# A 90-degree rotation: loads split over two queues, and one transpose per slab in place of two

## The chip, the cores and the metric

The kernel runs on one core of one Trainium2 chip (trn2). The metric is the device time of one execution in microseconds (us), lower is better. The profiled executions had a granted clock of 1.00. "The same" means a difference under 2%.

Names: SyncE and ScalarE issue transfers here and do nothing else. VectorE ("DVE" in the profile) does the transposes. "DMA" is the core's 16 DMA engines, which move the bytes of every transfer, whoever issued it. HBM is the chip's main memory and SBUF the core's own, where the tiles lie. The span is the profiled stretch, from the first to the last instruction.

## The reference

```python
def setup_inputs():
    batch, c, h, w = 32, 3, 256, 256
    return {"x": np.random.randn(batch, c, h, w).astype(np.float32)}

def reference(x):
    return np.rot90(x, k=-1, axes=(-2, -1)).astype(np.float32)
```

There are 96 planes of 256 x 256 float32, each rotated clockwise. There is no arithmetic: 25.17 MB go in and 25.17 MB come out.

## The kernel before

A slab is 128 partitions x 2048 float32 = 1 MiB, eight image rows per partition, so every partition's part of a slab is one contiguous 8 KiB run in HBM. There are 24 slabs. All 24 are loaded into tiles of their own. VectorE transposes slab `n` out of `units[n]` into `units[n - 1]`, which is free by then; one spare tile serves slab 0. The store goes out from there.

```python
    R = 8
    G = H // R
    n_slabs = B * C * G // P                     # 24
    N_UNITS = n_slabs + 1
    # ... ld_v, st_v: views of HBM as [n, p, 2048] with 8 KiB contiguous per partition (cut)
    pools = [ctx.enter_context(tc.tile_pool(name=f"unit{u}", bufs=1)) for u in range(N_UNITS)]
    units = [p.tile([P, R * W], fp32, name=f"u{u}") for u, p in enumerate(pools)]

    for n in range(n_slabs):
        nc.sync.dma_start(out=units[n], in_=ld_v[n])

    for n in range(n_slabs):
        t_in, t_out = units[n], units[n - 1]
        src = t_in.rearrange("p (r g c) -> p c r g", r=R, c=R)
        dst = t_out.rearrange("p (c g r) -> p c r g", c=R, r=R)[:, :, ::-1, ::-1]
        for h in range(2):
            cs = slice(h * R // 2, (h + 1) * R // 2)
            nc.vector.transpose(out=dst[:, cs], in_=src[:, cs])

        cuts = [0, W, R * W] if n == 0 else [0, R * W]
        for a, b in zip(cuts, cuts[1:]):
            nc.sync.dma_start(out=st_v[n][:, a:b], in_=t_out[:, a:b])
```

In the compiled program the framework gives the transfers eight completion semaphores in turn. A transfer that takes one again waits until the transfer that had it before has landed, so at most eight are in flight (the trace's issues and landings never show more).

## Time and profile before

| | before |
|---|---|
| median of 6 runs | 124.65 us (124.46 to 125.2) |
| span of the profiled execution | 122.9 us |
| VectorE busy | 95.6 us, 78% |
| DMA, middle 38 slices | nine tenths or more, 413 to 435 GB/s |
| VectorE's first start and last end | 5.65 us, 102.0 us |
| time outside the span (124.65 - 122.9) | 1.8 us |

First the page of the kernel before. The DVE and DMA rows have one digit for each fortieth of the span, in tenths of that slice; the GB/s row is what the DMA engines moved. In the group line (L53), "x48 | 95.6, 2057" is 48 instructions, 95.6 us busy in all, 2057 ns each; then come VectorE's idle time before them and what ended it. The last lines are the issues: count, size, median time from issue to landing.

```profile
span 122.9 us, 190 instructions
DVE  0199999999999999999999999999999992000000
DMA  3999999999999999999999999999999999999993
GB/s 83 416 427 429 429 424 421 427 427 419 413 419 427 427 421 421 424 424 413 424 414 429 427 429 427 429 429 427 421 427 427 427 429 427 427 427 427 427 435 165
q1 hardware_dynamic: 7056, 50.33, 98.0%
DVE 43%; issue 34%; DMA 4%; DVEq 2%
L53 DVE STREAM_TRANSPOSE u<-u 128x1024 f32<-128x1024 f32 x48 | 95.6, 2057 | 6.4 <-DMA u<-in_x_dram 5.6
...
u<-in_x_dram SPq DMA_DIRECT2D x24, 1024.0 KB, 19.9
out_dram<-u SPq DMA_DIRECT2D x23, 1024.0 KB, 19.5
```

Three things are to be seen. The DMA row is full from the second slice to the last but one, while the DVE row ends six slices early: the limit seems to be in the DMA engines. The chain of waits (the line "DVE 43%; issue 34% ...") names VectorE all the same. It is a trail of releases. And issue to landing is 19.9 us for a transfer that needs about 2.45 us at 427 GB/s: eight are queued.

The second view is the waits of SyncE's queue, total us, times, longest. Nearly all are waits for a landing, which is what a full queue looks like; only 0.6 us is for VectorE.

```profile
SPq L45 <- DMA u<-in_x_dram: 32.9, 16, 2.2
SPq L57 <- DMA out_dram<-u: 32.7, 17, 2.4
...
SPq L57 <- DMA u<-in_x_dram: 16.7, 8, 2.1
...
SPq L57 <- DVE u L53: 0.6, 2, 0.3
```

The third view is windows of the span: stretch, its length, VectorE busy (instructions), POOL busy, clock, DMA share (it may pass 1.00, since a packet is put into the window where it starts), GB/s.

```profile
20.00:40.00 20.00, 19.83 (x11) 0.00 (x0) 1.00 1.01 421
...
66.00:100.00 34.00, 33.72 (x18) 0.00 (x0) 1.00 1.01 427
100.00:118.00 18.00, 2.02 (x2) 0.00 (x0) 1.00 1.01 427
```

### The profile page before, as it was taken

What the parts mean: (1) busy time and instruction counts of PE and PEld (TensorE: products, weight loads), DVE (VectorE), ACT (ScalarE), POOL (GpSimd) and SP (SyncE); (2) the same over time, 40 slices, a digit from 0 to 9 for tenths busy, and PEclk for the clock granted to TensorE, in tenths of its full rate; (3) what the DMA queues carried; (4) which work ended last, traced back from release to release, by engine and by line L of the source; (5) the groups of instructions that cost most, each with busy time, mean ns of one, the idle gap of its engine ahead of it and who ended that gap; (6) DMA issues with size and microseconds to landing.
All of it is one profiled execution on the core that took longest, in us unless ns stands there. A gap on an engine that the chain in (4) does not pass through costs nothing.

```text
span 122.9 us, 190 instructions
## 1 busy us (share of the span) xinstructions
DVE 95.6 (78%) x48; POOL 0.2 (0%) x4
## 2 busy tenths in 40 slices
DVE  0199999999999999999999999999999992000000
POOL 0000000000000000000000000000000000000000
DMA  3999999999999999999999999999999999999993
GB/s 83 416 427 429 429 424 421 427 427 419 413 419 427 427 421 421 424 424 413 424 414 429 427 429 427 429 429 427 421 427 427 427 429 427 427 427 427 427 435 165
DMA packets 7058, 50.35 MB, mean 410 GB/s; under 512 B 784, under 2 KB 912, under 8 KB 1040
## 3 DMA queue, kind: packets, MB, share of 16 engines
q1 hardware_dynamic: 7056, 50.33, 98.0%
q14 instruction: 2, 0.02, 0.0%
HBM read 25.17 MB, written 25.17 MB: 410 GB/s over the span
## 4 chain that ended last, share of the span: by engine, by line
DVE 43%; issue 34%; DMA 4%; DVEq 2%
DVE u L53 43%; DMA u<-in_x_dram 4%; DVEq L83 2%
## 5 line engine op out<-in xcount | busy, mean ns | idle before, releaser
L53 DVE STREAM_TRANSPOSE u<-u 128x1024 f32<-128x1024 f32 x48 | 95.6, 2057 | 6.4 <-DMA u<-in_x_dram 5.6
L72 POOL MEMSET const-bfloat16-1.0<- 128x1 bf16 x1 | 0.1, 101 | 0.0
L72 POOL MEMSET const-uint8-127<- 128x1 uint8 x1 | 0.1, 101 | 0.0
L72 POOL MEMSET const-float32-0.0<- 128x1 f32 x1 | 0.1, 98 | 0.2 <-issue 0.2
L72 POOL MEMSET const-float32-1.0<- 128x1 f32 x1 | 0.1, 98 | 0.0
## 6 DMA issues: line engine op xcount, KB each, us to landing
u<-in_x_dram SPq DMA_DIRECT2D x24, 1024.0 KB, 19.9
out_dram<-u SPq DMA_DIRECT2D x23, 1024.0 KB, 19.5
out_dram<-u SPq DMA_DIRECT2D x1, 896.0 KB, 17.5
out_dram<-u SPq DMA_DIRECT2D x1, 128.0 KB, 17.9
```

The costliest lines, as they stand in the source:

```text
L53: nc.vector.transpose(out=dst[:, cs], in_=src[:, cs])
L72: nc = _bacc.Bacc("TRN2", target_bir_lowering=False, num_devices=1)
L83: with _tile.TileContext(nc) as tc:
```

## The change

The intent: issue the loads from two engines, so that neither waits for the other's issues, and halve the number of VectorE instructions.

```diff
     for n in range(n_slabs):
-        nc.sync.dma_start(out=units[n], in_=ld_v[n])
+        eng = nc.scalar if n % 2 else nc.sync
+        eng.dma_start(out=units[n], in_=ld_v[n])
 
     for n in range(n_slabs):
         # ... src, dst as before (cut)
-        for h in range(2):
-            cs = slice(h * R // 2, (h + 1) * R // 2)
-            nc.vector.transpose(out=dst[:, cs], in_=src[:, cs])
+        nc.vector.transpose(out=dst, in_=src)
```

## The prediction

> **What bounds the kernel now.** The DMA engines. The page's slice table shows them at nine tenths or more in 38 of 40 slices, moving 413 to 429 GB/s in nearly all; the queue table gives the one queue 98.0% of 16 engines' span. 50.33 MB at about 425 GB/s is 118.4 us of the 122.9 us span. The other 4.5 us are the start (first load issued at 0.73 us, landed 4.90 us later) and the last landing. VectorE is busy 95.6 us (78%). The chain of waits names VectorE with 43%, but VectorE waited only once, 5.6 us for the first load, and ends at 102.0 us, some 20 us early. The waits of SyncE's queue are nearly all for earlier landings (32.9 us for loads in front of loads, 32.7 and 16.7 us in front of stores) and only 0.6 us for VectorE: the framework rotates eight completion semaphores, so eight transfers are in flight, and 8 x 2.45 us (1 MiB at 427 GB/s) is the 19.9 us from issue to landing. All 24 loads go first (to about 62 us), then the stores.
>
> **What the change does.** No byte is added or removed. Twelve loads move to ScalarE's queue. The eight semaphores stay, now four for SyncE and four for ScalarE, so still eight in flight. An issue costs 0.33 us, and SyncE had nothing else to do: no gain on the path. The Trainium skill, "DMA: Bandwidth & Descriptors", section "Issuing engines are not separate DMA queues", says both issuers' transfers run on the same 16 engines and interleave, saving only issue time; the trace before agrees: one queue already fills them.
>
> - First load: slabs 0 and 1 share the rate, so slab 0 lands about one 1 MiB transfer (2.45 us) later; VectorE starts near 8.0 us instead of 5.65. Later slabs come at 4.9 us per pair against 8.1 us of work per pair: no second wait of weight.
> - One transpose per slab: two of 2.057 us (about 4.02 us per slab with their overlap) become one of about 4.05 us. VectorE, off the path, ends near 104.5 us.
> - The last store was issued at 102.4 us; now near 105 us. The queue then still holds about five stores (12 us or more), so no bubble follows.
> - Loads finish near 62 us on both queues, the stores queued behind SyncE's.
>
> On the critical path nothing changes but the rate of the engines while two queues interleave. Load slices averaged about 423 GB/s, store slices about 427. If two queues hide a gap between packets, the loads gain at most up to the 435 GB/s that the same page gives in "Where 436 GB/s comes from" (estimate: 25.17 MB, 59.5 to 57.9 us, 1.6 us); if interleaving costs, a similar loss.
>
> **Predicted: 124.5 us, range 123.3 to 125.7 us.** Chances: faster by over 2%: 0.04; within 2%: 0.92; slower by over 2%: 0.04.
>
> **What would show it.** DMA share still nine tenths in the middle 38 slices at 420 to 430 GB/s; two hardware queues, of about 37.7 and 12.6 MB; VectorE's first wait 7 to 8 us, 24 transposes of 4.0 to 4.1 us, end at 104 to 106 us with the DMA still full to the end; issue to landing still about 19 to 20 us for loads and stores.
>
> **What would make it wrong.** If the engines do not share evenly between the queues, in-order VectorE would wait for the slower queue's slabs, and stores with it; more than about 12 us of such waits would open a bubble at the end. If interleaved loads ran at under 405 GB/s, or loads mixed with stores lost rate, the loss could pass 2%. A gain over 2% needs over 435 GB/s or a shorter start.

## The result, and the profile after

| | before | after |
|---|---|---|
| median of 6 runs | 124.65 us (124.46 to 125.2) | 124.54 us (124.37 to 124.81) |
| ratio, 95% interval | | 0.9989 (0.9969 to 1.0009): the same |
| first slab landed after its issue | 4.90 us | 7.77 us |
| VectorE's first start, last end | 5.65, 102.0 us | 8.52, 104.3 us |
| VectorE, start to start per slab | 4.02 us | 3.99 us |
| first and last byte packet | 1.74, 121.60 us | 1.75, 121.69 us |

A ratio is the mean time of one kernel's fast runs over that of the other's of the same rounds, so it is not quite the ratio of the medians quoted. The last row is read from the trace's single DMA packets.

The page of the kernel after, the same lines:

```profile
span 122.9 us, 165 instructions
DVE  0029999999999999999999999999999999000000
DMA  4999999999999999999999999999999999999994
GB/s 77 395 427 432 427 421 427 424 419 421 419 424 424 419 421 427 421 419 419 427 415 430 427 427 432 427 427 427 427 427 429 427 427 427 427 427 427 427 427 189
q1 hardware_dynamic: 5328, 37.75, 73.6%
q10 hardware_dynamic: 1728, 12.58, 24.7%
DVE 78%; DMA 6%; issue 1%
L53 DVE STREAM_TRANSPOSE u<-u 128x2048 f32<-128x2048 f32 x24 | 95.0, 3960 | 9.3 <-DMA u<-in_x_dram 8.5
...
out_dram<-u SPq DMA_DIRECT2D x23, 1024.0 KB, 19.5
u<-in_x_dram SPq DMA_DIRECT2D x12, 1024.0 KB, 19.9
u<-in_x_dram ACTq DMA_DIRECT2D x12, 1024.0 KB, 19.9
```

There are now two queues, q1 (SyncE, 37.75 MB) and q10 (ScalarE, 12.58 MB), and their shares, 73.6% and 24.7%, add to 98.3% where one queue had 98.0%. The DMA row is as full as before. VectorE starts one slice later and ends 2.3 us later, still six slices before the end. Issue to landing is unchanged: still eight in flight. The chain of waits went from 43% to 78% VectorE while the time stayed the same. That rise is bookkeeping: in the list of the chain's pieces before, the stretches called "issue" (34% in all; one is 1.91 us long from 13.72 us) fall inside half-transposes that VectorE is working on (this one runs from 13.68 to 15.76 us). 43% and 34% together are about the 78% of the kernel after.

The waits of SyncE's queue and the windows of the kernel after:

```profile
SPq L57 <- DVE u L53: 2.4, 3, 1.8
```

```profile
20.00:40.00 20.00, 19.83 (x6) 0.00 (x0) 1.00 1.01 422
...
66.00:100.00 34.00, 33.72 (x9) 0.00 (x0) 1.00 1.01 428
100.00:118.00 18.00, 4.32 (x2) 0.00 (x0) 1.00 1.01 428
```

The loads run at 422 GB/s on two queues, at 421 on one; the stores at 428 and 427. Stores wait 2.4 us for VectorE in place of 0.6, and no bubble follows in the DMA row.

From the trace's packets, MB moved in each 10 us by queue, and the mean time of an 8 KiB packet in ns (worked out from the trace, not a view of the page):

```
us      before, q1      after, q1       after, q10
20-30   4.20  313.5     2.13  313.8     2.11  313.4
30-40   4.22  313.5     2.11  313.8     2.10  313.3
40-50   4.24  313.6     2.11  313.7     2.11  313.3
70-80   4.27  309.0     4.30  309.0     -
```

The engines share themselves evenly between the two queues, and a packet takes as long with two queues as with one. This is the whole result: the engines work through the same packets at the same pace.

### The profile page after: what moved, and what is told of

It reads as the page before. It is cut to its first block, busy times and chain, and to the rows that moved or that the text cites. A ratio compares the mean times of both kernels' runs of the same rounds, so it can differ in the third digit from the quotient of the medians.

```text
span 122.9 us, 165 instructions
## 1 busy us (share of the span) xinstructions
DVE 95.0 (77%) x24; POOL 0.2 (0%) x4
## 3 DMA queue, kind: packets, MB, share of 16 engines
q1 hardware_dynamic: 5328, 37.75, 73.6%
q10 hardware_dynamic: 1728, 12.58, 24.7%
## 4 chain that ended last, share of the span: by engine, by line
DVE 78%; DMA 6%; issue 1%
DVE u L53 78%; DMA u<-in_x_dram 6%
## 5 line engine op out<-in xcount | busy, mean ns | idle before, releaser
L53 DVE STREAM_TRANSPOSE u<-u 128x2048 f32<-128x2048 f32 x24 | 95.0, 3960 | 9.3 <-DMA u<-in_x_dram 8.5
## 6 DMA issues: line engine op xcount, KB each, us to landing
out_dram<-u SPq DMA_DIRECT2D x23, 1024.0 KB, 19.5
u<-in_x_dram SPq DMA_DIRECT2D x12, 1024.0 KB, 19.9
u<-in_x_dram ACTq DMA_DIRECT2D x12, 1024.0 KB, 19.9
```

The source lines that it names most:

```text
L53: nc.vector.transpose(out=dst, in_=src)
```

## The experiments

Theory: the 16 DMA engines are full and take the packets of both queues in turn, at an unchanged time per packet; VectorE has slack, and the later start and the shorter transposes both vanish in it. Rivals: (a) the two halves of the change have effects that cancel; (b) VectorE is the limit, as the chain of waits says; (c) the rate at which the bytes move is not the limit.

### Each half of the change alone

The split of the loads alone (edit against the kernel after):

```diff
-        nc.vector.transpose(out=dst, in_=src)
+        for h in range(2):
+            cs = slice(h * R // 2, (h + 1) * R // 2)
+            nc.vector.transpose(out=dst[:, cs], in_=src[:, cs])
```

> Only the loads' split over two queues; the transposes stay two per slab. My theory (the 16 DMA engines are full and share evenly between the queues, so the split moves no byte and hides no gap): 124.5 to 124.7 us, ratio to the kernel before 0.997 to 1.003; first transpose near 8.5 us as in the changed kernel, VectorE's last end near 105 us. Rival (the split wins or loses something that the single transpose hides in the full change): a ratio outside 0.995 to 1.005, with the opposite sign in the run that has the single transpose alone.

The single transpose alone:

```diff
-        eng = nc.scalar if n % 2 else nc.sync
-        eng.dma_start(out=units[n], in_=ld_v[n])
+        nc.sync.dma_start(out=units[n], in_=ld_v[n])
```

> Only the single transpose per slab; all loads stay on SyncE. My theory: ratio 0.997 to 1.003; first transpose at 5.65 us as before, 4.00 us per slab instead of 4.02, so VectorE ends near 101.5 us; the end does not move. Rival (two effects that cancel): ratio outside 0.995 to 1.005.

Measured, both correct: the split alone 124.82 us, ratio 1.0012 (0.9993 to 1.0031), VectorE from 8.39 to 104.8 us; the single transpose alone 124.71 us, ratio 0.9995 (0.9980 to 1.0010), VectorE from 5.59 to 101.4 us. From the timelines of the two runs (start, length), and then the chain of waits of the single transpose alone:

```profile
8.39 96.37 DVE L54 STREAM_TRANSPOSE u<-u 128x1024 f32<-128x1024 f32 x48 [8.39 <-DMA u<-in_x_dram]
5.59 95.81 DVE L52 STREAM_TRANSPOSE u<-u 128x2048 f32<-128x2048 f32 x24 [5.59 <-DMA u<-in_x_dram]
DMA 44%; DVE 36%; SPq 2%; issue 0%
```

Nothing of opposite sign cancels: each half is worth nothing within about 0.3%. The late start belongs to the split, the shorter pace (3.99 for 4.02 us per slab) to the single transpose. Rival (a) falls. The chain gives VectorE 36% here and 78% in the kernel after, for the same transposes at the same pace and the same time.

### An eighth of VectorE's transposing

Wrong result on purpose:

```diff
+    nc.vector.memset(units[n_slabs], 0.0)
-        nc.vector.transpose(out=dst, in_=src)
+        nc.vector.transpose(out=dst[:, 0:1], in_=src[:, 0:1])
```

> Wrong result on purpose: the changed kernel with only one eighth of every slab transposed, so VectorE's work falls from about 95 us to about 12 us, with all loads and stores as they are. My theory (VectorE has slack and the DMA engines bound the kernel): 124.3 to 124.7 us, ratio to the kernel before 0.996 to 1.003. Rival (the chain of waits is right that VectorE's 78% is the path): the time falls by far more than 2%, towards 30 to 60 us less.

Measured: 124.73 us, ratio 0.9997 (0.9982 to 1.0012). From the page of this run:

```profile
DVE 17.9 (15%) x25; POOL 0.2 (0%) x4
DVE  5022404304124042140430000000000000000000
DMA  4999999999999999999999999999999999999994
```

VectorE's busy time fell by 77 us (to 17.9, not to the expected 12: a short transpose took 0.67 us, and the added memset 1.8) and the time did not move. Rival (b) falls, and with it the reading of the chain's 78% as a share of the time that could be won.

### More work for VectorE: where the slack ends

The first two kernels added a transpose of a scratch tile ahead of each slab, of 160 and of 512 elements per partition (shown for the latter; scratch tiles cut):

```diff
+    nc.vector.memset(scr_a, 0.0)
+        nc.vector.transpose(out=scr_b, in_=scr_a)
         nc.vector.transpose(out=dst, in_=src)
```

> The changed kernel with one more transpose of 160 elements per partition on a scratch tile ahead of each slab, about 0.33 us, about 8 us in all. My theory of slack (VectorE may end as late as about 116 us before the last stores start late): VectorE ends near 112 us and the time stays 124.4 to 124.8 us. Rival (VectorE on the path): about 8 us longer, 132 us.

> The same with an extra transpose of 512 elements per slab, about 1.0 us, about 24 us in all. My theory: VectorE ends near 128.5 us, past the slack, so the last store is issued then and lands some 5 us later; 135 to 137 us in all, that is about 12 us longer for 24 us more work. Rival (VectorE on the path all along): about 148 us. Rival (VectorE never matters): 124.5 us.

Measured: 124.69 us (ratio 0.9999) and 124.70 us (ratio 1.0002, 0.9987 to 1.0017). The second expectation was missed, and the timeline shows why the run did not test what it was meant to. Columns: start, length, engine, line, operation, count.

```profile
1.42 5.19 DVE L57 STREAM_TRANSPOSE scr_b<-scr_a 128x512 f32<-128x512 f32 x7
8.58 3.96 DVE L58 STREAM_TRANSPOSE u<-u 128x2048 f32<-128x2048 f32 x1 [1.97 <-DMA u<-in_x_dram]
```

The scratch transposes depend on no load, so seven of them were scheduled into the wait for the first slab, and each took about 0.7 us, not 1.0. VectorE ended at 110.5 us, inside the slack (104.2 us in the first of the two). The next two kernels tie the extra work to the slab, with 256 and with 512 elements per partition (shown for the latter):

```diff
+        nc.vector.transpose(out=scr, in_=src[:, 0:2])
         nc.vector.transpose(out=dst, in_=src)
```

> The earlier two runs with extra work did not cross the slack: the scheduler put the scratch transposes into the wait for the first load, and VectorE ended at 104.2 and 110.5 us. Here the extra transpose reads the slab itself (256 strided elements per partition), so it can't run early; 0.5 to 0.7 us per slab. VectorE should end at 117 to 121 us. From the run with half the loads the time is VectorE's end plus 6.7 us once VectorE is last, so the edge lies at about 118 us: 124.6 to 127.8 us. Rival (VectorE never matters): 124.5 us with VectorE ending past 119 us.

> The same with 512 strided elements, 0.9 to 1.2 us per slab: VectorE should end at 126 to 133 us, and the time should be that end plus 6.7 us, 133 to 140 us; the DMA slices should fall under nine tenths near the end. Rival (VectorE never matters): 124.5 us. Rival (VectorE on the path all along): 124.5 us plus the whole extra work, 146 to 153 us.

Measured, both correct: with 256 elements 124.68 us, ratio 0.9990, VectorE ends at 111.0 us, earlier than expected, so this run too stays inside the slack. With 512 elements 128.45 us, ratio 1.0291 (1.0275 to 1.0307), VectorE ends at 121.8 us. The page, and the waits of SyncE's queue, of this last run:

```profile
DVE  0049999999999999999999999999999999999950
DMA  4999999999999999999999999999999999997735
GB/s 88 420 433 433 417 422 420 430 425 414 420 422 427 427 417 417 422 427 422 411 428 430 427 425 430 427 427 427 427 427 427 427 422 427 427 430 300 303 130 231
```

```profile
SPq L60 <- DVE u L56: 35.3, 9, 4.3
```

The DMA row now has holes in its last four slices, and stores wait 35.3 us for VectorE. The sizes of the expectations were off: 4.73 us per slab in place of about 4.9 to 5.2, and 128.45 us in place of 133 to 140. The trace shows why: the extra transpose adds 0.97 us, but what follows the slab's own now starts 3.76 us after it in place of 3.99, since it does not have to wait for the one just before (the section "Half the loads" comes back to this). With 256 elements it is 0.51 and 3.76 us. The rule in the expectation held: the time was VectorE's end plus 6.6 us (128.45 - 121.83), against 6.7 us in the run with half the loads below. So VectorE becomes the limit when it ends later than about 124.6 - 6.7 = 117.9 us (an estimate from these two runs). The kernel after ends at 104.3 us: some 13.6 us of slack. The kernel before ended at 102.0 us, so the change used 2.3 us of what was there.

### Half the loads

Wrong result: each loaded slab is transposed and stored twice.

```diff
-    for n in range(n_slabs):
+    for n in range(n_slabs // 2):
-        t_in, t_out = units[n], units[n - 1]
+        t_in, t_out = units[n // 2], units[12 + n % 13]
```

> Wrong result on purpose: the changed kernel with only twelve of the 24 loads, each loaded slab transposed and stored twice; 37.7 MB move in place of 50.3 MB. My theory: the DMA part would end near 92 us, so VectorE becomes the limit: first transpose at 8.5 us, 24 times 4.0 us, end near 104.5 us, then one last store of about 5 us: 111 to 113 us, 10% less than before for 25% fewer bytes, with DMA slices well under nine tenths in the later half. If the bytes were not the limit: no change, 124.5 us. If they were the only limit: 95 us.

Measured: 105.42 us, ratio 0.8458 (0.8445 to 0.8470). Page and the waits of SyncE's queue:

```profile
DVE  0007999999999999999999999999999999999900
DMA  3999999999999999999999999997756855945963
```

```profile
SPq L57 <- DVE u L53: 57.9, 18, 3.4
```

Taking bytes away does shorten the kernel, by 19 us, so rival (c) falls. Whether the engines themselves or the memory behind them set the rate is not told apart by this run; for the change it makes no difference, since both queues meet the same limit. As expected the time stops at VectorE: the DMA row is half empty in the last third and stores wait 57.9 us for VectorE. The size was off by about 6 us: VectorE took 3.76 us per slab, not 3.99, and ended at 98.7 us.

```profile
8.33 90.36 DVE L53 STREAM_TRANSPOSE u<-u 128x2048 f32<-128x2048 f32 x24 [8.33 <-DMA u<-in_x_dram]
```

In this kernel a transpose does not write the tile that the transpose just before it read, so it does not have to wait for it, and the trace has it start 0.16 us before the record of the one before ends. In both main kernels each slab's first transpose has to wait, and starts 0.035 us after that end. The kernel before shows both: the second half of a slab starts 0.13 us before the first half ends, the next slab's first half 0.035 us after the end.

### Loads and stores in one stretch

All loads on SyncE, all stores on ScalarE, a load written behind each store:

```diff
-    for n in range(n_slabs):
-        eng = nc.scalar if n % 2 else nc.sync
-        eng.dma_start(out=units[n], in_=ld_v[n])
+    AHEAD = 6
+    for n in range(AHEAD):
+        nc.sync.dma_start(out=units[n], in_=ld_v[n])
-            nc.sync.dma_start(out=st_v[n][:, a:b], in_=t_out[:, a:b])
+            nc.scalar.dma_start(out=st_v[n][:, a:b], in_=t_out[:, a:b])
+        if n + AHEAD < n_slabs:
+            nc.sync.dma_start(out=units[n + AHEAD], in_=ld_v[n + AHEAD])
```

> All loads on SyncE, all stores on ScalarE, written so that a store comes between the loads (six loads ahead), so loads and stores share the engines from about 12 us on. My theory: the engines stay at 420 to 428 GB/s and share evenly, so loads come at about 4.9 us per slab, VectorE catches up with them near 60 us and ends near 115 us in place of 104 us; the total stays within 2%: 124.5 to 127 us. Rival (reads mixed with writes lose rate): under 410 GB/s in the mixed part and over 127.5 us. Rival (mixing gains rate): over 435 GB/s and under 122 us.

Measured: 124.29 us, just under the expected range, ratio 0.9967 (0.9952 to 0.9982), correct. VectorE waited 18.5 us for loads in 15 places (5.7 us of it for the first) and ended at 113.8 us, and none of it cost anything, again inside the slack. The rate from the page:

```profile
GB/s 80 420 428 428 381 370 426 428 428 428 428 428 428 428 428 428 428 428 425 428 428 423 428 428 428 428 428 428 428 428 428 428 428 428 428 425 425 428 428 219
```

Where loads and stores run together the rate is 428 GB/s and a packet takes 309 ns, for loads too; where loads run alone it was, from about 20 us on, 421 to 423 GB/s and 313.5 ns, on one queue or on two. So the order of loads and stores moves the rate by about 1.4%, while the number of queues does not. Two slices near 12 to 18 us give part of it back (381 and 370 GB/s).

I put that dip down to too few transfers in flight and built a version to avoid it:

```diff
-    AHEAD = 6
+    AHEAD = 8
-        nc.sync.dma_start(out=units[n], in_=ld_v[n])
+        (nc.scalar if n % 2 else nc.sync).dma_start(out=units[n], in_=ld_v[n])
-        cuts = [0, W, R * W] if n == 0 else [0, R * W]
+        cuts = [0, R * W]
```

> A version meant to beat both: the first eight loads alternate between the two queues, so that eight are in flight from the start; after that loads on SyncE and stores on ScalarE with a load written behind each store, and the first store is whole. The mixed run had 428 GB/s and packets of 309 ns wherever loads and stores ran together, against 422 GB/s and 313.5 ns where loads ran alone, but lost rate in two slices near 12 to 18 us (381 and 370 GB/s), where too few transfers were in flight. Without that dip: 123.4 to 123.9 us, ratio 0.990 to 0.994. If the dip stays, or the fill comes from elsewhere: 124.2 us.

Measured: 124.28 us, ratio 0.9954 (0.9942 to 0.9967), correct. It is faster than the kernel before by about half a per cent (under the 2%, but the interval is clear of 1), while 0.6 to 1.0% had been expected: the dip stayed, so too few transfers in flight do not explain it here. The windows around it:

```profile
19.00:21.00 2.00, 1.97 (x2) 0.00 (x0) 1.00 1.03 430
21.00:23.00 2.00, 2.00 (x1) 0.00 (x0) 1.00 1.00 336
23.00:25.00 2.00, 1.97 (x2) 0.00 (x0) 1.00 1.01 426
```

From 21 to 23 us the DMA engines are as busy as ever (1.00) and move 336 GB/s: packets last longer, 400 to 720 ns for 29 of them in the trace, as the first stores join the loads. The engines were not short of work: eight transfers were in flight, three of them stores. (In the first mixed run it was five from 10 to 16 us, so a lack of work may have added to its dip.) The change from loads to stores shows in other kernels too, more faintly (384 GB/s in one slice with the longer rows below, 411 to 414 GB/s from 60 to 64 us in the kernel after). Why those packets are slow, and why loads alone take 313.5 ns after about the first 20 us, is open. VectorE reading and writing the same memory is an unlikely reason for the 313.5 ns: with an eighth of its transposing the loads still ran at 421 GB/s from 25 to 58 us. This version was not run in the same rounds as the kernel after; its lead over that is seen only through the kernel before (0.9954 against 0.9989).

### Longer rows

Wrong result: slabs of 2 MiB with 16 KiB per partition row. The core of the edit (the tiles become one tile, cut):

```diff
-    n_slabs = B * C * G // P
+    n_slabs = B * C * H // (P * 2 * R)
-    ld_v = ....rearrange("(n p r) w -> n p (r w)", p=P, r=R)
-    st_v = ....rearrange("(n p c) w -> n p (c w)", p=P, c=R)
+    ld_v = ....rearrange("(n p r) w -> n p (r w)", p=P, r=2 * R)
+    st_v = ....rearrange("(n p c) w -> n p (c w)", p=P, c=2 * R)
```

> Wrong result on purpose: slabs of 2 MiB with 16 KiB per partition row in place of 8 KiB, the same bytes and the same transposes. It asks whether the about 309 ns that an 8 KiB packet takes hold a fixed part. If they do[...], packets of 16 KiB take about 610 ns and the steady part falls by 1.3%, 1.5 us; but the first slab lands later (about 12.5 us) and the last one too: 123.3 to 125 us. If the packets stay at 8 KiB or the cost is all bytes: 124.5 to 126 us.

Measured: 123.08 us, a little under the expected 123.3 to 125 us, ratio 0.9870 (0.9852 to 0.9889). From the page:

```profile
DMA packets 3600, 50.33 MB, mean 415 GB/s; under 512 B 400, under 2 KB 528, under 8 KB 528
GB/s 146 394 432 432 432 432 432 432 432 432 432 421 427 427 432 421 427 432 432 421 384 432 432 432 427 432 427 432 432 427 432 432 432 432 432 432 432 432 432 178
```

A 16 KiB store packet takes 611 ns (the trace's median), where two of 8 KiB take 2 x 309 = 618: about 7 ns of a store packet do not depend on its length (an estimate from these two lengths), or 3.5 ns saved per 8 KiB. Load packets gained more: a mean of 614.6 ns from 30 to 58 us, where two of 8 KiB take 2 x 313.5 = 627, or 6 ns per 8 KiB. Besides the order of loads and stores this is the only edit here that made the kernel faster without leaving bytes out: by 1.3%, though its first slab lands so late that VectorE starts at 13.0 us. It is not a usable kernel. With eight rows per partition a plane fills 32 partitions and the result is right; with 16 rows it fills 16, and the result is wrong (relative error 1.41), presumably because the transpose's blocks then mix two planes. I found no arrangement with long rows on both sides and tried none with them on one side, so that stays open.

## Why the prediction was right

A forecast of no change can come out right by errors that cancel; the two halves, run alone, show that it did not here.

- **The limit.** Predicted: the DMA engines. Shown: VectorE's work cut to an eighth changes nothing (0.9997), a quarter of the bytes left out saves 15%, and 3.5 to 6 ns less per 8 KiB saves 1.3%. What in the path of the bytes sets the time of a packet was not tested.
- **Two queues on the same engines.** The Trainium skill, page "DMA: Bandwidth & Descriptors", section "Issuing engines are not separate DMA queues", says that transfers of both issuers run on the same 16 engines and interleave; the section "Queues, rings and completion order" says that an engine takes the queues in turn, packet by packet. The trace agrees: 2.11 and 2.11 MB in the same 10 us, 313 to 314 ns per packet with one queue and with two. It shows equal shares; the order of packets on one engine was not looked at. The possible 1.6 us from a gap hidden between packets did not come: 422 GB/s against 421.
- **The first slab.** Predicted 2.45 us later, VectorE near 8.0 us. Measured 2.87 us later and 8.52 us. The step was right and its size a little short; the slack took it, as the split alone showed.
- **The single transpose.** Predicted about 4.05 us per slab; it is 3.99, against 4.02. VectorE's end was predicted at 104 to 106 us and came at 104.3.
- **The margin.** Predicted: about five stores still queued when the last is issued, so that more than about 12 us of waits would open a bubble. Eight transfers were in flight then (the last store issued at 104.4 us, the last byte at 121.7), so the margin was put a little low. The run with 512 extra elements per slab puts the edge near 117.9 us, 13.6 us behind VectorE's end.
- **In flight.** Predicted: still eight, about 19 to 20 us to landing. Measured 19.5 and 19.9.

What the prediction did not see is that the order of loads and stores, and not the number of queues, moves the engines' rate a little.

## What to carry to other kernels

Before you spread transfers over more queues, read the DMA row and the time of a packet: where the engines are full, a second queue only deals out the same packets, and work saved on an engine with slack is worth nothing. A chain of waits can name an engine that is not the limit (VectorE's share was 43%, 78% and 36% at the same time here); take its work away, or add some until the time moves, to learn what it is worth. Work that you add as a probe must depend on the data that it is to delay, or it may be scheduled into an idle stretch; and read from the trace what it really added, for it can take away a wait (0.97 us of work lengthened a slab by 0.74 here).

## What the Trainium skill lacked or had wrong

- "DMA: Bandwidth & Descriptors", section "Where 436 GB/s comes from", says without a condition that for transfers between HBM and SBUF the HBM side (about 358 GB/s) binds. With this one core at work the loads ran at 421 to 423 GB/s and the stores at 427 to 428. The page "HBM Reference", section "Specifications (TRN2)", says that a core alone streams at about 425, which these runs agree with. The first page says so too, but in another section; the sentence itself should name its case.
- The page "DMA: Bandwidth & Descriptors" explains the fixed cost of a packet with an example of 256 bytes and gives none near 8 KiB. Here it still showed: store packets took 309 ns for 8 KiB and 611 ns for 16 KiB, 427 against 432 GB/s.
- No page that I read tells loads from stores in rate. Here an 8 KiB load packet took 313.5 ns while loads ran alone (from about 20 us on) and 309 ns beside stores, and when the first stores joined a stream of loads the rate was 336 GB/s for about 2 us.
- "VectorE: DVE Perf Modes", section "The DRAIN you can't avoid", says of eight copies that the semaphore between them "costs nothing extra here", and also that an instruction that is not held starts earlier; the section measures no transposes. Here transposes of a slab followed each other in 3.99 us where each had to wait for the one just before, and in 3.76 us where it did not.
